# Four edits in a two-block transformer kernel: the rare places of a MoE expert inside its pair, earlier splits, one gate product, no GpSimd gemv

## The chip, the cores and the metric

The kernel runs on one core of one Trainium2 chip. The time is the device time of one execution in microseconds, the median of several. The core has a matrix engine (TensorE, PE in the profile, with its weight loads as PEld), a vector engine (DVE), a scalar engine (ACT), GpSimd (POOL) and a synchronisation engine (SP), which here issues nearly all loads. Each engine works off its own queue of instructions in order and waits on semaphores; 16 DMA engines move the data.

## What is computed

256 tokens of width 1024 pass two blocks of two layers each. Only the parts that the change touches are shown, in short:

```python
mod = c_act @ w_ada + b_ada                      # 6 x 1024 numbers for each layer
x = x + g1 * (mixer(norm(x)) @ w_out)            # layers of block 1: attention, convolution, spatial gating
x = x + g2 * peer_ffn(norm(x))                   # block 1: 16384 small experts, 8 heads x 16 chosen for a token
...
x = x + g1 * mix                                 # block 2: GLA in layer 0, LRU in layer 1
x = x + g2 * grouped_moe(norm(x))                # block 2: 16 experts of width 512, 2 for a token

def grouped_moe(h, ...):
    ...
    for e in range(16):
        he = silu(t @ w_gate[e]) * (t @ w_up[e])
        out = out + combine[:, e:e + 1] * (he @ w_down[e])
```

## The kernel before

The engines' queues are written out by hand: an instruction stands on its engine where the Python code calls it, and no scheduler moves it. Weights come through a `Stream`: `raw` and `fill` use slots of 1 MB, `release` gives one back and `pump` at once issues the next loads on SP (L71 and L74). Each load counts up one of eight semaphores (DMAHW0 to DMAHW7), so eight are in flight at most. For matmuls at full precision a weight is split into a high part (cast on ACT, L108) and a low part (subtraction on DVE, L113), and three matmuls are made. All matmuls are recorded at L267.

**Mixer and gemv.** The six vectors `mod` of a layer come from a product of the weights `in_ada` with one vector, in halves of 128x1024, by `gemv` (L321 to L333): one DVE instruction with a running sum (L333) for each half. For layer 0's parts 16 to 39, which are made while its first mixer runs, the first half of each of 12 tiles is instead multiplied on GpSimd (L330) and summed on ACT (L331). The first mixer runs the same code in both layers. Its DVE work begins with L609, and its output product is added to `x` at L474; then come a reciprocal (L414) and the scaled norm (L420, L433).

**PEER.** The 16384 experts are gone through in tiles of 128 by matmuls of split weights (`in_pdown`, then `in_pup`). Beside them a generator (`peer_select`) puts DVE and ACT work between the tiles: the choice of the experts, then 64 gate steps of four tokens. A step is a comparison of 128x1024 f16 (L970), two products of 128x512 (L976) that multiply the place's one-hot rows by their weights, matmuls of the result, and their evacuation (L944, L947).

**MoE.** Tokens are sorted to the 16 experts by one-hot matmuls. `experts` goes through eight pairs p of two experts, 64 places for each: loads of the gate weights (`in_mg`, four of 1 MB), up (`in_mu`) and down (`in_md`). In a pair: the gate half, the up half, `hidden`, the scatter of the pair before, `turn`, the down product, `parts`. Where an expert has over 64 tokens, blocks under `If(rv[p] > 64)` run the second 64 places: L1755 and L1758 behind the gate half, L1770 behind the up half, L1782 behind the down product. In the profiled run the block of L1782 is entered once in 16, in pair 2 of layer 1. After the eight pairs the scatter and `rstd` follow, and then, where an expert has over 128 tokens, L1826 would run the whole of `experts` again for the places from 128 and from 192, with a stream of its own (`S2`). No count here is over 128. Then `S.passed()` and `S.fill(1)` make the first two splits of the next stage (two L108, two L113).

An `If` is a branch on every engine that has instructions in the block. On the way around it an engine counts up the semaphores that the block would have counted up, and first waits for what the block's counts build on.

Of the kernel before, what the change touches and what calls it, by code (L numbers as in the profile page):

```python
# [7 lines left out]
F32 = mybir.dt.float32  # L8
# [4 lines left out]
OP = mybir.AluOpType  # L13
# [132 lines left out]


class LazyFour:


    def __init__(self, S):
        self.S, self.got = S, []

    def __getitem__(self, i):
        while len(self.got) <= i:
            self.got.append(self.S.raw())
        return self.got[i]


class Kern:  # L160
# [678 lines left out]
    def peer_select(self, qT, keys, st):  # L839
# [122 lines left out]
        for t0 in range(0, 256, 4):  # L962
# [3 lines left out]
            R = O[:, 0:512].rearrange("p (a j t) -> p a j t", a=2, t=2)  # L966
            C = O[:, 512:].rearrange("p (s a j t) -> p s a j t", s=2, a=2, t=2)
            bc = lambda i, n: (TT[:, t0 // 4, 4 * i:4 * (i + n)].rearrange("p (c t) -> p c t", t=2)[:, :, None, :]
                               .to_broadcast([128, 2 * n, 128, 2]))
            TX(O[:, :1024].rearrange("p (c j t) -> p c j t", c=4, t=2),  # L970
               self.io4[:, None, :, 0:2].to_broadcast([128, 4, 128, 2]), bc(0, 2), op=OP.is_equal)
# [3 lines left out]
            for n in (1, 0):  # L975
                TX(C[:, n], C[:, 0], bc(3 - n, 1), op=OP.mult)  # L976
# [518 lines left out]

    def route(self, h, hf, ht):
# [79 lines left out]
        cnt = self.sm.tile([1, 13], mybir.dt.int32, name="cnt")  # L1576
# [11 lines left out]
        def counts():  # L1588
            nc.vector.tensor_reduce(cnt[:, 0:8].rearrange("p (g b) -> p g b", b=2), swap(pr[0:1, 32:48]), op=OP.max, axis=AX)
            nc.vector.tensor_reduce(cnt[:, 8:12], pr[0:1, 32:48].rearrange("p (a b) -> p a b", b=4), op=OP.max, axis=AX)  # L1590
            nc.vector.tensor_reduce(cnt[:, 12:13], pr[0:1, 32:48], op=OP.max, axis=AX)
# [10 lines left out]
    def experts(self, S, base, ht, w, rk, g2, r, first=None):  # L1602
# [7 lines left out]
        P2 = self.fw6[:, :512].rearrange("p (t e s) -> p t e s", t=2, e=4)  # L1610
        PT2 = self.fw6[:, 512:768]
        if base:
            rk, old = self.scr(32), rk
            nc.vector.tensor_scalar(rk, old, float(-base), None, op0=OP.add)
        r3 = rk.rearrange("p (t e) -> p t e", t=2)
        w3 = w.rearrange("p (t e) -> p t e", t=2)
        xs = [t.bitcast(F32) for t in self.pair()]
        cw, cw2 = self.scr(8), self.scr(1)
        sg, he, hT, he2 = self.scr(512), self.scr(512), self.scr(512), self.scr(512)
        rv = None  # L1620
# [31 lines left out]
        def half(ws, x, c0):  # L1652

            ps = self.bank()
            for i in range(2):
# [5 lines left out]
                if first is None:  # L1661
                    for e in range(2):
                        S.release(ws[2 * i + e][0])
# [387 lines left out]
```

## Time and profile before

| | |
|---|---|
| median of three runs | 2714.59 us (2713.24 to 2715.59) |
| the profiled execution, its own time | 2714.08 us |
| its span, from the first to the last instruction | 2712.3 us |
| mean granted TensorE clock | 0.983 |
| busy: PE, DVE, ACT, POOL | 2567.9, 1892.2, 1173.2, 65.7 us |
| moved by the DMA engines | 658.32 MB, 243 GB/s in the mean |
| PEER of layer 0, then mixer 1 of layer 1 | about 165 to 980, to 1105 us |
| PEER of layer 1, then GLA | to 1915, to 2060 us |
| MoE of layer 0, LRU, MoE of layer 1 | 2075 to 2311, to 2420, 2440 to 2700 us |

Each row of the profile that follows names a line of the kernel, an engine and the tiles written and read; "idle before, releaser" is the time in which the engine did nothing ahead of it, and what ended that. SPq, PEq, DVEq and PEldq are the sequencers of the engines: their branches and semaphore waits, which are not counted as busy. The PE clock is in parts of full speed. The DMA share is the mean busy share of the 16 engines. A row of the windows has the window, its length, the busy time of PE, PEld, DVE, ACT and POOL (instructions in brackets), the PE clock, the DMA share and GB/s.

### The profile page before, as it was taken

How to read it: one execution, taken by the hardware profiler on the slowest of the kernel's cores; microseconds unless marked ns; L12 is line 12 of the kernel's file. 1: busy time of each engine (PE TensorE's matmuls, PEld its weight loads, DVE VectorE, ACT ScalarE, POOL GpSimd, SP SyncE). 2: the span in 40 equal slices, each digit the busy share in tenths (PEclk: the TensorE clock that was granted, in tenths of full speed). 3: DMA queues.
4: the chain of work that ended last, by engine and by line, in shares of the span. 5: the costliest groups of instructions: out<-in, count | busy, mean ns of one | idle time of the engine just before them, and what ended most of it. 6: DMA issues, size and time to landing. Idle time of an engine off the chain costs nothing. (4 is left out here: it accounts for less than half of the span.)

```text
span 2712.3 us, 42904 instructions
## 1 busy us (share of the span) xinstructions
PE 2567.9 (95%) x17017; PEld 2144.5 (79%) x17017; DVE 1892.2 (70%) x3505; ACT 1173.2 (43%) x1861; POOL 65.7 (2%) x62
## 2 busy tenths in 40 slices
PE   6899999999999999999999999999998998888997
PEld 5889999998888889999999888888895443874433
DVE  7868999996798977599899957888753121761222
ACT  3554555544544455454554345445643111651111
POOL 3300000000000000000000000000000000000000
PEclk8899999999999999999999999999999999999999
DMA  9562444445899963515444458988526999459795
GB/s 390 202 230 76 156 171 156 156 155 192 304 398 365 354 240 125 179 48 174 171 159 153 154 204 335 379 343 313 190 91 242 415 417 413 163 188 373 297 405 230
DMA packets 99812, 658.32 MB, mean 243 GB/s; under 512 B 11604, under 2 KB 13140, under 8 KB 26232
## 3 DMA queue, kind: packets, MB, share of 16 engines
q1 hardware_dynamic: 96480, 649.44, 62.9%
q10 hardware_dynamic: 3096, 5.68, 0.6%
q8 instruction: 154, 2.52, 0.4%
q14 instruction: 82, 0.67, 0.1%
HBM read 654.03 MB, written 1.05 MB: 242 GB/s over the span
## 5 line engine op out<-in xcount | busy, mean ns | idle before, releaser
L267 PE MATMUL bank<-hthi,whi 128*128 128x256 f32 x2920 | 848.2, 290 | 19.1 <-ACT whi L108 9.5
L267 PE MATMUL bank<-htlo,whi 128*128 128x256 f32 x2920 | 834.4, 286 | 5.6 <-DVE htlo L428 3.7
L267 PE MATMUL bank<-hthi,wlo 128*128 128x256 f32 x2920 | 832.1, 285 | 5.9 <-DVE wlo L113 5.8
L267 PEld LDWEIGHTS bank<-hthi,whi 128*128 128x128 f32 x2920 | 563.1, 193 | 32.1 <-ACT whi L108 9.7
L267 PEld LDWEIGHTS bank<-htlo,whi 128*128 128x128 f32 x2920 | 562.9, 193 | 11.1 <-DVE htlo L428 8.4
L267 PEld LDWEIGHTS bank<-hthi,wlo 128*128 128x128 f32 x2920 | 562.3, 193 | 8.0 <-DVE wlo L113 7.8
L108 ACT CAST whi<-r 128x1024 fp32r<-128x1024 f32 x331 | 347.4, 1050 | 486.9 <-PE bank L267 461.3
L113 DVE TENSOR_TENSOR wlo<-arena,whi 128x1024 fp32r<-128x1024 f32 (+1 forms) x322 | 392.3, 1222 | 199.4 <-ACT whi L108 194.5
L113 DVE TENSOR_TENSOR wlo<-r,whi 128x1024 fp32r<-128x1024 f32 x331 | 404.6, 1224 | 113.1 <-ACT whi L108 111.4
L108 ACT CAST whi<-arena 128x1024 fp32r<-128x1024 f32 (+1 forms) x322 | 332.7, 1037 | 306.8 <-PE bank L267 299.9
L267 PE MATMUL bank<-whi,hthi 128*128 128x512 f32 (+1 forms) x1088 | 421.7, 388 | 2.4 <-ACT hthi L306 2.4
L267 PE MATMUL bank<-wlo,hthi 128*128 128x512 f32 (+1 forms) x1088 | 421.8, 388 | 0.5 <-DVE wlo L113 0.5
L267 PE MATMUL bank<-whi,htlo 128*128 128x512 f32 (+1 forms) x1088 | 421.7, 388 | 0.2
L267 PEld LDWEIGHTS bank<-whi,hthi 128*128 128x128 f32 x1088 | 204.2, 188 | 43.9 <-ACT hthi L306 2.8
L267 PEld LDWEIGHTS bank<-whi,htlo 128*128 128x128 f32 x1088 | 204.2, 188 | 42.1 <-DVE htlo L307 1.1
L267 PEld LDWEIGHTS bank<-wlo,hthi 128*128 128x128 f32 x1088 | 204.2, 188 | 42.0 <-DVE wlo L113 1.1
L267 PE MATMUL bank<-arena 128*64 128x512 f32 (+6 forms) x856 | 176.0, 480 | 19.9 <-ACT arena L1674 12.4
L333 DVE SCALAR_TENSOR_TENSOR arena<-arena 128x1024 f32<-128x1024 f32 x136 | 163.6, 1240 | 0.0
L267 PEld LDWEIGHTS bank<-arena 128*64 128x64 f32 (+3 forms) x848 | 85.2, 165 | 85.6 <-issue 59.8
L1667 DVE SCALAR_TENSOR_TENSOR arena<-bank,arena 128x512 f32<-128x512 f32 x17 | 12.8, 752 | 176.4 <-PEq L1770 163.6
L947 DVE SCALAR_TENSOR_TENSOR arena<-bank,arena 128x416 f32<-128x416 f32 (+23 forms) x128 | 123.1, 962 | 0.0
L267 PE MATMUL bank<-arena,hthi 128*64 128x512 f32 x456 | 120.5, 595 | 2.2 <-ACTq L1782 0.8
(358 smaller groups left out, 2693.5 us busy)
## 6 DMA issues: line engine op xcount, KB each, us to landing
r<-in_pdown SPq DMA_DIRECT2D x110, 1024.0 KB, 4.9
arena<-in_pup SPq DMA_DIRECT2D x81, 1024.0 KB, 6.5
arena<-in_ada SPq DMA_DIRECT2D x72, 1024.0 KB, 6.9
arena<-in_mu SPq DMA_DIRECT2D x56, 1024.0 KB, 12.5
arena<-in_md SPq DMA_DIRECT2D x54, 1024.0 KB, 12.1
r<-in_pup SPq DMA_DIRECT2D x47, 1024.0 KB, 5.5
arena<-in_mg SPq DMA_DIRECT2D x40, 1024.0 KB, 11.5
r<-in_ada SPq DMA_DIRECT2D x24, 1024.0 KB, 7.0
```

Source lines behind the costliest of these rows:

```text
L108: k.nc.scalar.copy(hi[:, :n], ap)
L113: self.k.nc.vector.tensor_sub(lo[:, :n], ap, hi[:, :n].bitcast(F32))
L267: self.nc.tensor.matmul(o, l, r, start=start, stop=stop)
L333: self.nc.vector.scalar_tensor_tensor(w, w, 1.0, cb, op0=OP.mult, op1=OP.mult, accum_out=o)
L947: nc.vector.scalar_tensor_tensor(o[:, :, :j - j0], p4[:, :, j0:j], 1.0 / GSC, o[:, :, :j - j0], op0=OP.mult, op1=OP.mult)
L1667: nc.vector.scalar_tensor_tensor(o, pu, c, s, op0=OP.mult, op1=OP.mult)
```

## The change

There are four edits.

1. The block L1826 behind the pairs is gone. A new function `rest` computes the places over 128 of one pair's two experts, 128 at a time, with its own stream `S2` on the four slots that held the pair's down weights. It stands under `If(rv[p] > 128)` (L1824 of the changed kernel) inside the last block of each pair, `over(p)` (L1819 there, L1782 before). The other lines are L1792, L1795 and L1806 for L1755, L1758 and L1770. 12 counts are loaded into registers, not 13.
2. `S.passed()` and `S.fill(1)` move into `ahead()`, which is called in the last pair ahead of its down product. In layer 1 nothing is behind it to be split.
3. The gate step's two products become one of 128x1024, which reads one row block twice and writes two; the comparison writes the first and the third of three row blocks (L959, L963 for L970, L976).
4. `gemv` makes both halves on DVE (L321 for L333); the calls of GpSimd and ACT are not reached any more.

```diff
@@ gemv @@
-            self.gemv(l, m, cb, l == 0 and 16 <= m < 40)
+            self.gemv(l, m, cb)
@@ peer_select @@
-            R = O[:, 0:512].rearrange("p (a j t) -> p a j t", a=2, t=2)
-            C = O[:, 512:].rearrange("p (s a j t) -> p s a j t", s=2, a=2, t=2)
...
-            TX(O[:, :1024].rearrange("p (c j t) -> p c j t", c=4, t=2),
-               self.io4[:, None, :, 0:2].to_broadcast([128, 4, 128, 2]), bc(0, 2), op=OP.is_equal)
+            A = O.rearrange("p (s a j t) -> p s a j t", s=3, a=2, t=2)
+            R, C = A[:, 0], A[:, 1:3]
+            O2 = O.rearrange("p (s b) -> p s b", s=3)
...
+            TX(O2[:, 0::2], self.io4[:, None, :, 0:2].to_broadcast([128, 4, 128, 2]), bc(0), op=OP.is_equal)
             yield self.GC
             if len(pend) == 2:
                 evac(*pend.popleft())
-            for n in (1, 0):
-                TX(C[:, n], C[:, 0], bc(3 - n, 1), op=OP.mult)
+            TX(O2[:, 1:3], O2[:, 2:3].to_broadcast([128, 2, 512]), bc(2), op=OP.mult)
@@ experts @@
+        def rest(p, ws, o, x):
+
+            S2 = Stream(self, 3)
+            S2.free.extend(q for q, _ in ws)
+            self.add_rest(S2, l, p)
+            S2.pump()
...
+            for e in range(2):
+                c = 2 * p + e
+                nc.vector.tensor_scalar(rk2, r3[:, :, c:c + 1], -128.0, None, op0=OP.add)
...
+                def part():
+                    ps = self.bank()
+                    for i in range(2):
+                        q, v = S2.raw()
+                        for k in range(4):
+                            self.mm(ps, x[:, 4 * i + k, :], v[:, k * 512:(k + 1) * 512], i + k == 0, i + k == 4)
+                        S2.release(q)
+                    return ps
+
+                nc.scalar.activation(he2, part(), AF.Silu)
+                hidden(part(), cw2, he2, he2)
...
+                parts(y, o)
+                scatter(o, PT2)
...
             turn(he)
+            if p == 7:
+                ahead()
             ws = take()
             parts(down(ws), ys[p % 2])
-            if first is not None:
-                with over(p):
-                    turn(he2)
-                    o = ys[(p + 1) % 2]
-                    parts(down(ws), o)
-                    scatter(o, PT2)
+            with over(p):
+                turn(he2)
+                o = ys[(p + 1) % 2]
+                parts(down(ws), o)
+                scatter(o, PT2)
+                with self.tc.If(rv[p] > 128):
+                    rest(p, ws, o, x if j else x2)
+                    if j == 0:
+                        onehot(P2, 4 * g, 4, 64)
+                        gather(P2, x2)
             give(ws)
@@ moe @@
-        with self.tc.If(rv > 128):
-            S2 = Stream(self, 3)
-            S2.free.extend(S.lent[:2])
-            for base in (128, 192):
-                self.scr_at = [list(q) for q in at]
-                self.add_experts(S2, l)
-                S2.pump()
-                self.experts(S2, base, ht, w, rk, g2, r)
-        S.passed()
-        S.fill(1)
+        def ahead():
+            S.passed()
+            S.fill(1)
+
+        r = self.experts(S, l, ht, w, rk, g2, low, counts, weights, cnt, ahead)
```

The order of the instructions shows what this makes of the queues. SP, MoE of layer 0, around the last block of pair 6; in_md are the down weights of pair 7, in_lwin belongs to the LRU. Before:

```order
L74 DMA arena<-in_md 128x2048 [waits DMAHW7_49,PE_49]
L1782 COMPARE_AND_BRANCH
L1782 UNCONDITIONAL_BRANCH x2
L74 DMA arena<-in_md 128x2048 [waits DMAHW0_49,PE_49]
L74 DMA arena<-in_md 128x2048 [waits DMAHW1_49,PE_49]
L74 DMA arena<-in_md 128x2048 [waits DMAHW2_49,PE_49]
L74 DMA arena<-in_lwin 128x2048 [waits DMAHW3_49,PE_49]
L1758 COMPARE_AND_BRANCH
```

and the same place now, from the end of the block on (its twelve loads stand ahead of these rows):

```order
L74 DMA arena<-in_md 128x2048 [waits DMAHW2_49,PE_49]
L74 DMA arena<-in_md 128x2048 [waits DMAHW3_49,PE_49]
L1824 UNCONDITIONAL_BRANCH
L1824 UNCONDITIONAL_BRANCH [waits DMAHW0_49,DMAHW1_49,DMAHW2_49,DMAHW3_49,DMAHW4_49,DMAHW5_49,DMAHW6_49,DMAHW7_49]
L1819 UNCONDITIONAL_BRANCH [waits DMAHW0_49,DMAHW1_49,DMAHW2_49,DMAHW3_49,DMAHW4_49,DMAHW5_49,DMAHW6_49,DMAHW7_49]
L74 DMA arena<-in_md 128x2048 [waits DMAHW4_49,PE_49]
L74 DMA arena<-in_md 128x2048 [waits DMAHW5_49,PE_49]
L74 DMA arena<-in_md 128x2048 [waits DMAHW6_49,PE_49]
L74 DMA arena<-in_lwin 128x2048 [waits DMAHW7_49,PE_49]
L1795 COMPARE_AND_BRANCH
```

The way around L1782 had no wait on SP; each way around L1819 and L1824 now waits for all eight load semaphores, in every pair.

DVE, PEER of layer 0, two gate steps (L947/L935 is an evacuation, L113 the split of an expert tile, L1023/L1010 a product with the gates). Before:

```order
L970 TENSOR_TENSOR w_94<-io_88,TT 128x1024
L113 TENSOR_TENSOR wlo<-r_93,whi 128x1024
L1023 TENSOR_TENSOR arena<-arena,gt 128x2x108
L947 SCALAR_TENSOR_TENSOR arena<-bank,arena 128x4x86
L976 TENSOR_TENSOR w_94<-w_94,TT 128x512 x2
```

and now:

```order
L959 TENSOR_TENSOR w_94<-io_88,TT 128x2x512
L113 TENSOR_TENSOR wlo<-r_93,whi 128x1024
L1010 TENSOR_TENSOR arena<-arena,gt 128x2x108
L935 SCALAR_TENSOR_TENSOR arena<-bank,arena 128x4x86
L963 TENSOR_TENSOR w_94<-w_94,TT 128x1024
```

Nothing moves here but the two products, which are one.

DVE, the last pair of the MoE of layer 0, now (L462 is the scatter of pair 6, L295 evacuates the down product):

```order
L462 SCALAR_TENSOR_TENSOR x<-bank,adac_79,x 128x256 x8
L113 TENSOR_TENSOR wlo<-arena,whi 128x1024 x2
L295 TENSOR_TENSOR fa_19837<-bank,fa_19837 128x512 x2
L1819 COMPARE_AND_BRANCH
L295 TENSOR_TENSOR fa_19837<-bank,fa_19837 128x512 x2
```

Before, the two L113 stood behind L414 and L1826. The skipped part of L1819 grows on PE from some 40 instructions to some 240, on DVE from about 13 to 51, on ACT from 5 to 30. On DVE of the first mixer, layer 0, each L333 that had its other half on GpSimd is now two, four of them ahead of the first L609, seven between it and the first L474, and one between L414 and L420.

## Rows read from the trace of the kernel before

**Rows 1.** Windows, first PEER layer: us, busy (instructions) by engine, PEclk, DMA share, GB/s.
```profile
500.00:620.00 120.00, 116.56 (x1071) 113.84 (x1069) 118.55 (x185) 53.07 (x112) 0.00 (x0) 1.00 0.43 150
```

**Rows 2.** Waits of PE, whole run: engine, line, waited for, us in total, times, longest.
```profile
PE bank L267 <- DVE w L976: 12.3, 14, 3.2
```

**Rows 3.** Windows, first mixer of layer 0 and of layer 1.
```profile
76.40:154.50 78.10, 65.83 (x473) 61.31 (x473) 67.78 (x101) 39.32 (x93) 27.53 (x14) 0.85 0.53 198
1028.80:1089.20 60.40, 59.72 (x473) 56.28 (x472) 46.27 (x86) 32.04 (x79) 5.23 (x5) 0.92 0.34 123
```

**Rows 4.** Windows, MoE: layer 0, then layer 1 around pair 2.
```profile
2200.00:2230.00 30.00, 28.02 (x136) 10.67 (x138) 5.96 (x12) 2.93 (x5) 0.00 (x0) 1.00 1.02 418
2500.00:2530.00 30.00, 30.00 (x169) 14.70 (x166) 5.37 (x13) 3.33 (x6) 0.00 (x0) 1.00 0.74 283
2530.00:2560.00 30.00, 27.99 (x138) 10.86 (x138) 7.86 (x18) 4.12 (x7) 0.00 (x0) 1.00 0.65 247
```

**Rows 5.** Waits of PE in the MoE of layer 0, for loads.
```profile
PE bank L267 <- DMA arena<-in_mu: 2.2, 2, 1.4
PE bank L267 <- DMA wloraw<-in_mu: 1.6, 1, 1.6
```

**Rows 6.** Groups of DVE by shape, PEER of layer 0: busy us, mean ns, idle before.
```profile
L976 DVE TENSOR_TENSOR w<-w,TT 128x512 f16<-128x512 f16 x128 | 54.0, 422 | 2.2
L970 DVE TENSOR_TENSOR w<-io,TT 128x1024 f16<-128x1024 f16 x64 | 43.8, 685 | 0.2 <-PE bank L267 0.2
```

**Rows 7.** Timeline of DVE behind the first mixer: start, us, line, operation.
```profile
161.27 1.20 DVE L333 SCALAR_TENSOR_TENSOR r<-r,arena 128x1024 f32<-128x1024 f32 x1
162.40 0.08 DVE L333 DVE_READ_ACCUMULATOR r<-r,arena 128x1 f32 x1
```

**Rows 8.** Timeline of DVE, end of the MoE of layer 0.
```profile
2311.73 0.17 DVE L414 RECIPROCAL arena<-arena 128x2 f32<-128x2 f32 x1 [1.66 <-ACT arena L413]
2316.06 2.36 DVE L113 TENSOR_TENSOR wlo<-arena,whi 128x1024 fp32r<-128x1024 f32 x2 [4.17 <-DVEq L1826]
...
2319.10 0.87 DVE L433 SCALAR_TENSOR_TENSOR arena<-x,gs,bank 128x256 f32<-128x256 f32 x2 [0.59 <-PE bank L267]
```

**Rows 9.** Timeline of DVE, end of the MoE of layer 1.
```profile
2705.57 3.22 DVE L1916 SCALAR_TENSOR_TENSOR arena<-x,vec,bank 128x256 f32<-128x256 f32 x8 [4.60 <-PE bank L267]
```

**Rows 10.** SP's issues behind pair 6 of layer 0, and their us to landing.
```profile
2274.05 4.12 SPq L74 DMA_DIRECT2D arena<-in_md  x4
2280.34 3.96 SPq L74 DMA_DIRECT2D arena<-in_lwin  x3
...
arena<-in_md SPq DMA_DIRECT2D x1, 1024.0 KB, 17.4
arena<-in_lwin SPq DMA_DIRECT2D x1, 1024.0 KB, 17.3
```

**Rows 11.** Group of the page: the cast of a split.
```profile
L108 ACT CAST whi<-r 128x1024 fp32r<-128x1024 f32 x331 | 347.4, 1050 | 486.9 <-PE bank L267 461.3
```

**Rows 12.** Timeline of PE, the down product of pair 7, layer 0 and layer 1.
```profile
2294.30 7.09 PE L267 MATMUL bank<-arena 128*64 128x512 f32 x32 [0.74 <-ACT arena L1674]
...
2683.37 7.09 PE L267 MATMUL bank<-arena 128*64 128x512 f32 x32 [0.74 <-ACT arena L1674]
```

**Rows 13.** Instructions of L1826: count, ns min/median/max, first and last start.
```profile
L1826 SPq EVENT_SEMAPHORE  x16: 17/17/17, 2311.4 to 2682.9; - x16
...
L1826 PEldq COMPARE_BRANCH  x2: 3696/4868/6041, 2310.7 to 2699.7; - x2
```

**Rows 14.** Windows, SP's drain at L1826 in layer 0.
```profile
2312.00:2316.00 4.00, 0.00 (x0) 0.00 (x0) 0.00 (x0) 1.99 (x2) 0.00 (x0) 0.74 0.48 195
2316.00:2319.00 3.00, 1.99 (x7) 1.83 (x8) 2.44 (x3) 0.00 (x0) 0.00 (x0) 0.50 0.03 8
2319.00:2322.00 3.00, 3.00 (x15) 2.38 (x14) 2.66 (x7) 1.50 (x4) 0.00 (x0) 0.71 0.76 273
```

**Rows 15.** Waits of SP behind that drain.
```profile
SPq L74 <- DVE gs L420: 1.8, 1, 1.8
```

More of the change, by code (lines that the diff above doesn't have):

```diff
@@ L1600, in route, with experts @@
         return low, counts, weights, wp, rk, cnt
-    def experts(self, S, base, ht, w, rk, g2, r, first=None):
+    def experts(self, S, l, ht, w, rk, g2, low, counts, weights, cnt, ahead):
         nc = self.nc
@@ L1736, in experts @@
         onehot(Ps[0], 0, 4, 0)
-        if first is not None:
-            for i in (1, 2, 3):
-                first[0](i)
+        for i in (1, 2, 3):
+            low(i)
         gather(Ps[0], xs[0])
@@ L1747, in experts @@
             nc.scalar.activation(sg, ps, AF.Silu)
-            if p == 0 and first is not None:
-                first[1]()
-                first[2]()
-                rv = [nc.values_load(first[3][0:1, i:i + 1], min_val=0, max_val=256,
-                                     skip_runtime_bounds_check_because="a count of 256 tokens") for i in range(13)]
-            if first is not None:
-                if j == 0:
-                    with over(8 + g):
-                        onehot(P2, 4 * g, 4, 64)
-                        gather(P2, x2)
-                with over(p):
-                    nc.scalar.activation(he2, half(ws, x2, j * 128), AF.Silu)
-                    gather_w(P2, 4 * g, j, 1, cw2)
+            if p == 0:
+                counts()
+                weights()
+                rv = [nc.values_load(cnt[0:1, i:i + 1], min_val=0, max_val=256,
+                                     skip_runtime_bounds_check_because="a count of 256 tokens") for i in range(12)]
+            if j == 0:
+                with over(8 + g):
+                    onehot(P2, 4 * g, 4, 64)
+                    gather(P2, x2)
+            with over(p):
+                nc.scalar.activation(he2, half(ws, x2, j * 128), AF.Silu)
+                gather_w(P2, 4 * g, j, 1, cw2)
             give(ws)
@@ L1768, in experts @@
                 onehot(Ps[(g + 1) % 2], 4 * g + 4, 4, 0)
-            if first is not None:
-                with over(p):
-                    hidden(half(ws, x2, j * 128), cw2, he2, he2)
-                    transposed(P2, j, 1, PT2)
+            with over(p):
+                hidden(half(ws, x2, j * 128), cw2, he2, he2)
+                transposed(P2, j, 1, PT2)
             give(ws)
@@ L1778, in experts @@
             turn(he)
+            if p == 7:
+                ahead()
             ws = take()
             parts(down(ws), ys[p % 2])
-            if first is not None:
-                with over(p):
-                    turn(he2)
-                    o = ys[(p + 1) % 2]
-                    parts(down(ws), o)
-                    scatter(o, PT2)
+            with over(p):
+                turn(he2)
+                o = ys[(p + 1) % 2]
[3 more added lines that the diff above has]
+                    rest(p, ws, o, x if j else x2)
+                    if j == 0:
+                        onehot(P2, 4 * g, 4, 64)
+                        gather(P2, x2)
             give(ws)
@@ L1791, in experts @@
         scatter(ys[1], PTs[1][:, 1, :], ss)
-        self.rstd(ss, r)
-        return None if first is None else rv[12]
+        return self.rstd(ss)
     def moe(self, l, h, hf, g2):
```

70 lines of the change are left out of this document (43 added, 27 removed).

## Prediction

> **What bounds the kernel now.** I read the trace stage by stage, because the change touches three stages with different limits. First the busy time in a window of the first PEER layer, in which the gate steps run beside the expert matmuls, and what PE waits for there: DVE is busy 118.55 of 120 us and PE has lost 3.4 [rows 1]; PE's waits for a gate product are 12.3 us over both layers [rows 2]. DVE is the bound, barely. Second, the first mixer, which runs twice on the same work, in layer 0 with GpSimd multiplying beside it and in layer 1 without: from its first L609 to its first L474 it takes 78.1 us and 60.4 [rows 3]. In layer 1 PE is busy 59.72 us of that, so PE is the bound; in layer 0 DVE is busy 21.5 us longer and PE idles 12. Third, the MoE: the DMA engines are full (share 1.02, 418 GB/s) while PE is busy 28.02 of 30 us [rows 4] and has waited for loads only 2.2 + 1.6 us in the whole of layer 0 [rows 5]. Both are at their limit, and the loads have almost no lead over their use. Keep that in mind: what the DMA engines lose in this stage, PE soon loses too. The profiled run took 2714.08 us, its span 2712.3; the median of the runs is 0.5 us above it.
>
> **Gate product (two L976 become one).** The two products of a step take 422 ns each; the comparison L970 has 1024 f16 elements and takes 685 [rows 6]. One product of 1024 at L970's price saves 2 x 422 - 685 = 159 ns, and by an estimate 30 more for one start fewer: 0.19 us in each of 64 steps a layer. Some 45 of them lie in the saturated stretch: 8.5 us, more than the 6.2 us a layer that PE waits. The wait goes and no more, because then PE is the bound: **-12.3** for both layers. Bounds: -14, if the stretch itself quickens a little; and if the product with a repeated operand ran at the 1.20 us which an f32 operation of 1024 takes [rows 7], 0.36 us more per step, +32 for 45 steps twice.
>
> **Gemv.** GpSimd's and ScalarE's part goes; 12 L333 come to DVE in mixer layer 0 at 1.20 + 0.08 us [rows 7]. By the order four of them stand before the 78.1 us, seven inside, one behind. Inside: +9.0 of DVE work. Of the 21.5 us by which DVE is busier there than in layer 1, seven L333 that it has already make another 9.0; the other 12.5 are operations that take longer while GpSimd works, and they go. DVE's busy time so ends at 67.8 - 12.5 + 9.0 = 64.3 us, still above PE's 60: DVE is the bound, with 10.3 us of gaps now [rows 3], half of which I take as filled. The stretch then takes 64.3 + 5.2 = 69.5, 8.6 less. The four in front lie where PE is busy with the input product and cost an estimated 0.8 in all. The twelfth stands between the mixer and its norm beside the one at 161.27, 1.3 us of bare path. I take **-6.5**, between -12 (gaps all filled) and +3 (none filled, the four in front bare).
>
> **End of a MoE layer.** The skipped L1826 costs, from the reciprocal to the next scaling, 2319.10 - 2311.73 = 7.4 us in layer 0 [rows 8], of which about 1 is the chain's own: -6.4, with the two splits (2.36 us at 2316.06) inside it. In layer 1 DVE waits 4.60 [rows 9], about 0.8 of it its own: -3.8. The splits don't vanish: they move ahead of the evacuation of the last pair's down product. Their load, the first lwin, is issued at 2280.34 and takes 17.3 us, the last md (the end of the four issues that begin at 2274.05) at 2277.85 and 17.4 [rows 10]; so it lands 2.4 us later. A cast of 1.05 [rows 11] and the two subtractions, 3.4 us, follow, while the product is ready 1.8 us (a quarter of 7.09, [rows 12]) after the last md. Once PE waits for that md, the evacuation is held 2.4 + 3.4 - 1.8 = 4.0 us. Sum: -6.4 + 4.0 - 3.8 = **-6.2**. Bounds: -10.2 (splits hidden) and 0.
>
> **The If inside each pair.** This part decides. The loads of the rare case used to be issued inside L1826 alone, once a layer. Now they stand inside every pair's last If (L1819, nested L1824), and the way around it on SP has, as the order shows, waits for all eight load semaphores: SP can issue nothing until every load in flight has landed. L1826 did this twice; its 16 waits on SP lie between 2311.4 and 2682.9 [rows 13]. What one such drain costs is there to read: the DMA share falls from 2312 to 0.48, 0.03 and 0.76 [rows 14], which is 4 x 0.52 + 3 x 0.97 + 3 x 0.24 = 5.7 us lost; 1.8 of it SP waited for something else [rows 15]. So **3.9 us** each. Behind the waiting SP are queued the other md loads of the next pair and its mg loads, and PE waits for those. Bounds of one: 2.1 (the tail alone, 4 x 0.52) and 5.7.
>
> How many count? In layer 0 seven, pairs 0 to 6; behind pair 7's there are only loads of the LRU. Against them stands the lead at the end: the last md lands at 2277.85 + 17.4 = 2295.2, and its quarter of the product starts at 2294.30 + 5.3 = 2299.6 [rows 10, 12], 4.4 us: 7 x 3.9 - 4.4 = 22.9. In layer 1 pair 2 is the one whose block runs; PE is busy there without a gap and the DMA share falls to 0.74 and 0.65 [rows 4], so pairs 0 to 2 are absorbed. Pairs 3 to 6 count, against a lead of 2688.7 - 2682.9 = 5.8 by the same reckoning [rows 12, 13]: 4 x 3.9 - 5.8 = 9.8. Together **+32.7**; bounds 12.9 (at 2.1 each) and 52.5 (at 5.7).
> The Trainium skill, "DMA: Bandwidth & Descriptors", section "Anatomy of one DMA", gives a fixed cost of about 2.0 us per DMA, most of it completion, measured for DMAs of GpSimd. By it the drains would make 7 x 2.0 - 4.4 + 4 x 2.0 - 5.8 = 11.8, and the whole sum would come out near 2704. The row has in it also the spread of the 16 engines' ends, so I go by the row.
>
> **Longer skips.** The last If on PE now jumps over some 240 instructions where it was 40. A far jump took PE's sequencer 3.7 and 6.0 us at L1826, 4.9 in the mean [rows 13]. The sequencer reaches the branch while the 7.09 us of matmuls [rows 12] still run, and where PE then waits for loads the rest is covered; only pair 7 of a layer has no such cover. I take a quarter of the mean for these two: **+2.5**, between 0 and 15 skips at 2.4 (half of it) = 36. The jumps on DVE and ACT go with it; 12 counter loads instead of 13 are nothing.
>
> **Sum.** -12.3 - 6.5 - 6.2 + 32.7 + 2.5 = +10.2: 2714.1 + 10.2 = 2724.3, with the 0.5 to the median **2725 us**, slower by 0.4%. About 0.2%, 5.4 us, is what a measurement here can tell from no change.
>
> **Rivals.**
> *A drain costs its tail only* (2.1 us): the next loads' start overlaps the stragglers. Then +12.9 for the drains, in all -9.6: 2705. For it: nothing but eight short steps lies between the last landing and the next issue. Against it: [rows 14] shows 3 us with almost no transfer. The skill's 2.0 us would lead to the same. 0.15.
> *The drains are hidden anyway*: PE, at 28 of 30 us with waits for ACT and DVE besides, is the real bound. Then the other parts alone, with the splits hidden: -12.3 - 6.5 - 10.2 + 2.5 = -26.5: 2688. For it: 3.8 us of load waits in a layer [rows 5]. Against it: a share of 1.02 leaves no room to catch up. 0.10.
> *PE's skips are bare*: with the queues full, code comes later than at L1826. From the point where the fetch outlasts the matmuls still queued, each pair pays; at 1.6 us in 15 pairs, +24 instead of 2.5: 2746. Against it: it would fall into the same waits as the drains. 0.12.
> *The wide product is slow* (1.20 us): +32 instead of -12.3: 2769. Against it: L970 repeats an operand too and is fast. 0.04.
> The forecast has the remaining 0.59, in itself from 2707 to 2742.
>
> **How the numbers follow.** The range 2696 to 2747 takes in the forecast with its bounds of drain, the cheap drain and the bare skips; it leaves out the hidden drains and the slow product. Slower (above 2720): 0.40 of the forecast's 0.59, 0.12 and 0.04, in all 0.56. Faster (below 2709.2): the hidden drains 0.10, most of the cheap drain 0.13, and 0.04 of the forecast, 0.27. The same: the rest, 0.17.
>
> **What would show it.** In the changed profile: SP's own waits at L1819 and L1824 in every pair, over 100 us in both layers; a DMA share below 0.95 in the MoE windows, with a hole after each drain; PE waiting for in_mg, in_mu and in_md some 25 us in layer 0 against 3.8; pairs of about 34 us. The gate step's wait gone from PE's waits; mixer layer 0 at about 70 us; no 7.4 us from reciprocal to scaling at the end of the MoE. The forecast is wrong if the MoE windows keep a share of 1.0, or if SP is past its waits long before the last load lands.

## The result, and the profile of the changed kernel

| | before | changed |
|---|---|---|
| median, us | 2713.91 (2712.57 to 2715.59) | 2739.77 (2734.67 to 2748.68) |
| ratio | | 1.0093, 95% interval 1.0079 to 1.0108 |
| profiled execution: span, us | 2712.3 | 2745.6 |
| its mean granted TensorE clock | 0.983 | 0.978 |

The change makes the kernel 25.9 us slower; 10.2 were forecast. The profiled execution of the changed kernel is the longest of its four, so its stages stand about 9 us above the median.

**The stages.** I compare the time at which one instruction of each stage starts in the two profiled executions. From the norm behind the first mixer to the last product of PEER, the first PEER layer gives 3.9 us back and the second 4.0; the first mixer with its norm 2.3; GLA loses 1.6. The MoE of layer 0, from PE's first matmul behind the blocks of its first gate half to the reciprocal, takes 261.0 us for 229.6, and behind it 6.4 are won; the MoE of layer 1, by the same marks, loses 20.8 and then wins 3.8. Nearly all of the loss is in the two MoE layers.

The windows of that stretch of layer 0, before, changed, and without the skipped block (the experiment e1_no_rest, below); columns as in [rows 1].
```profile
2082.10:2311.70 229.60, 206.93 (x1079) 96.17 (x1079) 50.08 (x105) 29.09 (x52) 0.20 (x1) 1.00 1.01 413
```
```profile
2072.70:2333.70 261.00, 222.80 (x1081) 103.63 (x1081) 52.44 (x108) 30.90 (x54) 0.20 (x1) 0.95 0.90 360
```
```profile
2071.30:2300.90 229.60, 207.25 (x1081) 96.38 (x1081) 52.44 (x107) 31.11 (x54) 0.20 (x1) 1.00 1.01 414
```
Two losses show at once. The DMA share falls from 1.01 to 0.90, as forecast for the drains. The granted clock falls from 1.00 to 0.95, and this no part of the forecast had.

The instructions of the last If (L1819) in the changed kernel, as [rows 13] show them of L1826: count, ns min/median/max, first and last start; and SP's waits there in layer 0 and layer 1 (us in total, times, longest).
```profile
L1819 SPq EVENT_SEMAPHORE  x120: 17/17/17, 2083.6 to 2724.5; - x120
...
L1819 PEldq COMPARE_BRANCH  x16: 73/6116/6316, 2086.3 to 2724.1; - x16
```
```profile
SPq L1819 <- SPq L1819: 118.0, 46, 7.6
...
SPq L1819 <- SPq L1819: 101.0, 23, 16.5
```
SP drains its queue in each of 15 pairs: 120 waits, eight each. PE's sequencer takes 6.1 us in the median for a branch that took 0.337 before (73 is the one pair that enters the block, and does not jump):
```profile
L1782 PEldq COMPARE_BRANCH  x17: 73/337/357, 2095.6 to 2686.0; - x17
...
L1782 PEldq EVENT_SEMAPHORE  x15: 51/51/51, 2100.1 to 2690.5; - x15
```

What PE waits for in the MoE of layer 0 now, beside the 2.2 and 1.6 us of [rows 5]:
```profile
PE bank L255 <- DVEq L1795: 8.5, 4, 2.3
PE bank L255 <- PEq L1819: 7.3, 3, 3.0
PE bank L255 <- ACT arena L1663: 5.7, 8, 0.7
PE bank L255 <- DVEq L1819: 3.7, 1, 3.7
PE bank L255 <- PEq L1795: 3.6, 6, 1.7
PE bank L255 <- issue: 3.3, 1, 3.3
PE bank L255 <- DMA arena<-in_md: 2.5, 2, 1.4
```
The waits stand at branches, not at loads. A wait for several semaphores is put down to the last of them, so the rows name the place, pair by pair behind L1819, and not safely the culprit; the experiments had to tell it.

The other places. The gate product, first PEER layer, by shape, and what PE waits for there (before: 6.1 us in this layer, of the 12.3 of [rows 2]); the window that answers to [rows 1], and the stretch of the first mixer in layer 0 from its first L597 to its first L462, which answers to the first of [rows 3]:
```profile
L959 DVE TENSOR_TENSOR w<-io,TT 128x1024 f16<-128x1024 f16 x64 | 44.0, 687 | 1.2 <-PE bank L255 1.1
L963 DVE TENSOR_TENSOR w<-w,TT 128x1024 f16<-128x1024 f16 x64 | 43.9, 687 | 0.0
```
```profile
PE bank L255 <- DVE w L963: 3.1, 2, 2.6
```
```profile
500.00:620.00 120.00, 116.89 (x1087) 115.11 (x1086) 118.30 (x162) 53.20 (x115) 0.00 (x0) 1.00 0.45 158
77.27:149.60 72.33, 63.69 (x473) 58.85 (x471) 62.56 (x117) 31.07 (x79) 5.80 (x6) 0.88 0.55 199
```
The product costs 687 ns, L970's price as taken; the further 30 ns that were to fall away with one start stand in no row. DVE is as busy as before (118.30 us for 118.55), and half of PE's wait stays.

DVE at the end of the MoE, as [rows 8] and [rows 9]: layer 0, then layer 1.
```profile
2333.65 0.17 DVE L402 RECIPROCAL root<-root 128x2 f32<-128x2 f32 x1 [1.66 <-ACT root L401]
2334.62 0.87 DVE L421 SCALAR_TENSOR_TENSOR arena<-x,gs,bank 128x256 f32<-128x256 f32 x2 [0.74 <-PE bank L255]
...
2739.01 3.22 DVE L1949 SCALAR_TENSOR_TENSOR arena<-x,vec,bank 128x256 f32<-128x256 f32 x8 [0.80 <-PE bank L255]
```
The 7.4 us from the reciprocal to the first scaling are 1.0, and the 4.60 are 0.80.

### The profile page after: what moved, and what is told of

The parts are those of the page before. It is cut to its first block, busy times and chain, and to the rows that moved or that the text cites. A ratio compares the mean times of both kernels' runs of the same rounds, so it can differ in the third digit from the quotient of the medians.

```text
span 2745.6 us, 42858 instructions
## 1 busy us (share of the span) xinstructions
PE 2590.7 (94%) x17017; PEld 2155.7 (79%) x17017; DVE 1866.0 (68%) x3399; ACT 1160.7 (42%) x1837; POOL 31.5 (1%) x50
## 3 DMA queue, kind: packets, MB, share of 16 engines
q1 hardware_dynamic: 96480, 649.44, 62.6%
## 5 line engine op out<-in xcount | busy, mean ns | idle before, releaser
L113 DVE TENSOR_TENSOR wlo<-arena,whi 128x1024 fp32r<-128x1024 f32 (+1 forms) x322 | 387.5, 1207 | 206.1 <-ACT whi L108 205.3
L113 DVE TENSOR_TENSOR wlo<-r,whi 128x1024 fp32r<-128x1024 f32 x331 | 403.3, 1220 | 127.8 <-ACT whi L108 126.6
L321 DVE SCALAR_TENSOR_TENSOR arena<-arena 128x1024 f32<-128x1024 f32 x144 | 171.0, 1226 | 0.0
L255 PE MATMUL bank<-arena,htlo 128*64 128x512 f32 x368 | 115.1, 622 | 18.5 <-DVEq L1795 8.5
## 6 DMA issues: line engine op xcount, KB each, us to landing
arena<-in_mg SPq DMA_DIRECT2D x40, 1024.0 KB, 11.8
```

The costliest lines, as they stand in the source:

```text
L113: self.k.nc.vector.tensor_sub(lo[:, :n], ap, hi[:, :n].bitcast(F32))
L255: self.nc.tensor.matmul(o, l, r, start=start, stop=stop)
L321: self.nc.vector.scalar_tensor_tensor(w, w, 1.0, cb, op0=OP.mult, op1=OP.mult, accum_out=o)
```

## The experiments

Two theories stood against each other. **Drains**: SP's waits starve PE of weights, and the long jump is covered. **Skips**: PE's jump over 240 instructions ends after the matmuls queued ahead of it, and every pair pays. The diffs are against the changed kernel unless said otherwise; "e1" is e1_no_rest.

### Taking the block apart

**e1_no_rest**: the pair's last block without the places over 128.
```diff
-                with self.tc.If(rv[p] > 128):
-                    rest(p, ws, o, x if j else x2)
...
```


> The changed kernel without the block under If(rv[p] > 128): the places over 128 of an expert are left out. Every other edit stays. Both theories, the drain of SP and the longer skips, expect the whole loss to go: from the stage times of the changed kernel the gate product gave 8, the mixer 2.3 and the ends of the MoE about 10 us, so some 2694 us (2690 to 2700). SP's waits at L1819 and a PE branch of 6 us there should both be gone. If a part of the loss lies elsewhere (splits held in pair 7, GLA), it stays above 2700.

Measured: 2691.77 us, ratio to before 0.9913 (0.9896 to 0.9930). So the block that is never entered costs 2739.77 - 2691.77 = 48.0 us, and the other edits win 23.9 against the 2715.66 us of the kernel before as measured beside e1. The profile has pairs of 30.3 and 28.3 us by turns again, as before.

**e3_loads_only**: the block holds its 12 loads and no work. SP drains, PE's jump is short.
```diff
-                    rest(p, ws, o, x if j else x2)
...
+                    S2 = Stream(self, 3)
+                    S2.free.extend(q for q, _ in ws)
+                    self.add_rest(S2, l, p)
+                    S2.pump()
+                    for _ in range(12):
+                        S2.release(S2.raw()[0])
```


> The block under If(rv[p] > 128) holds only its twelve loads, no work (the places over 128 are left out). SP's way around has the eight waits, the jumps of PE, DVE and ACT are as short as before. Drain theory: 25 to 35 us above e1, near the changed kernel; DMA share about 0.9 in the MoE. Skip theory: within 3 us of e1. Mixed: 15 to 25 above e1.

Measured: 2727.44 us, 1.0042 (1.0027 to 1.0056): 35.7 over e1.
```profile
L1819 SPq EVENT_SEMAPHORE  x120: 17/17/17, 2082.7 to 2706.8; - x120
...
L1819 PEldq COMPARE_BRANCH  x16: 73/334/352, 2085.2 to 2706.4; - x16
```
By the profiled execution, which is 37.4 us longer than e1's, the eight pairs of layer 0 take 22.7 us more than in e1 (from the start of one down product to that of the next), those of layer 1 take 7.0 more, and the end of layer 0 a further 6.1: pair 7's product waits for its last loads (9.8 us for 7.1), then its evacuation is held behind the two splits (PE stands 3.72 us for 1.60), and the lower clock takes the remaining 1.3. The splits wait for the first lwin. PE's branch is at its 0.334 us, and the clock over the whole run is 0.984.

**e2_rest_no_loads**: the block keeps its matmuls and vector work, but takes the pair's own weights; no load, so no drain.
```diff
-            S2 = Stream(self, 3)
...
+            turn_ws = iter(list(ws) * 3)
...
-                        q, v = S2.raw()
+                        _, v = next(turn_ws)
```


> The block under If(rv[p] > 128) keeps its matmuls, vector work and length, but its weights are the four down tiles that the pair holds, not loads of its own (the places over 128 would come out wrong). The way around has no waits of SP, the jumps of PE, DVE and ACT are as long as in the changed kernel. Drain theory: as without the block, within 3 us of e1. Skip theory: all of the loss stays, 2735 to 2740. Mixed, as the pairs' +2.3 us in the first pairs suggest: 12 to 18 us above e1.

Measured: 2722.36 us, 1.0024 (1.0012 to 1.0036): 30.6 over e1, in both layers alike (pairs +16.8 and +15.3). Drain and skip are each nearly as dear alone; together they cost 48.0, not 66.3.

### Which engine's skip

**e5_pe_only**: the block holds 200 matmuls and nothing else.
```diff
-                    rest(p, ws, o, x if j else x2)
...
+                    for _ in range(50):
+                        ps = self.bank()
+                        for f in range(4):
+                            self.mm(ps, hT[:, f * 128:(f + 1) * 128], ws[f][1][:, 0:512], f == 0, f == 3)
```


> The block under If(rv[p] > 128) holds 200 matmuls and nothing else (the places over 128 are left out), so PE's jump is about as long as in the changed kernel, those of DVE, ACT and SP as short as in e1. If PE's jump is the cost of e2 (30.6 us above e1): 20 to 30 us above e1 (2712 to 2722), with PE branches of 6 us at L1819. If it is the jumps of DVE and ACT: within 3 us of e1.

**e6_vec_only**: 40 DVE and 25 ACT instructions instead.
```diff
+                    for _ in range(40):
+                        nc.vector.tensor_scalar(rk2, r3[:, :, 2 * p:2 * p + 1], -128.0, None, op0=OP.add)
+                    for _ in range(25):
+                        nc.scalar.copy(PT2, P2[:, 0, 0:4, :].rearrange("p e s -> p (e s)"))
```


> The block under If(rv[p] > 128) holds 40 small instructions of DVE and 25 copies of ACT and nothing else (the places over 128 are left out). PE's jump is short, those of DVE and ACT are as in the changed kernel. If PE's jump is the cost of e2: within 3 us of e1 (2689 to 2695). If DVE's and ACT's: 20 to 30 above it. A share of both: 5 to 15.

**e8_pe_short**: as e5_pe_only with `range(12)`, 48 matmuls.

> The block under If(rv[p] > 128) holds 48 matmuls and nothing else (the places over 128 are left out): about twice the jump of the kernel before, a quarter of the changed one's addition. If the cost has a threshold, that the target must be fetched anew once it is far enough: either 0.34 us at the branch and no loss (within 2 us of e1), or 6 us and the loss of e5. If it grows with the length: a quarter of e5's loss, 5 to 8 us.

Measured: 2716.69 (1.0010, 1.0000 to 1.0020), 2691.33 (0.9922, 0.9906 to 0.9939) and 2694.36 (0.9926, 0.9910 to 0.9943): 24.9, -0.4 and 2.6 over e1. The kernel before took 2713.47 us beside these three and 2715.66 beside e1, so -0.4 and 2.6 are not clear of nothing, and 24.9 is. It is PE's jump that costs, 24.9 of e2's 30.6, and not those of DVE and ACT by themselves; where e2's other 5.7 lie was not traced. The cost doesn't grow in proportion: a quarter of the matmuls costs a tenth. PE's branch of L1819 in e5_pe_only, then in e8_pe_short:
```profile
L1819 PEldq COMPARE_BRANCH  x16: 73/6002/6257, 2085.7 to 2690.4; - x16
```
```profile
L1819 PEldq COMPARE_BRANCH  x16: 73/337/3312, 2083.2 to 2673.1; - x16
```
Over 48 matmuls the branch takes 0.337 us, once 3.3; over 200 it takes 6.0 in nearly all pairs. What it does in that time stands in the DMA view. First the window of the first far jump in e5_pe_only (branch from 2085.7, window to 2092.2), then that of a near jump in e1 (0.34 us from 2115.1, window to 2121.1):
```profile
q1 hardware_dynamic: 380, 2.74, 100.6%
q8 instruction: 1, 0.02, 0.9%
```
```profile
q1 hardware_dynamic: 346, 2.49, 99.9%
q8 instruction: 1, 0.02, 1.1%
```
Each brings one packet on the instruction queue, behind a queue of loads that is full (the near jump of e1's first pair, 0.2 us, brings none). Both packets start some 3.6 to 3.8 us behind the start of the branch and have landed 1.0 to 1.1 us later. The near branch has long ended by then. The far one ends at 2091.7, 1.4 us behind the landing of its packet, which lies in this window (2089.2 to 2090.3):
```profile
q1 hardware_dynamic: 54, 0.43, 96.1%
q8 instruction: 1, 0.02, 5.6%
```
The rule holds without an exception here: in the fourteen traces PE's sequencer takes over 1.5 us for 80 branches behind 2040 us, and every one ends 1.3 to 1.7 us behind the landing of such a packet. So a near jump stays in code that the sequencer has, and a far one waits for code to be loaded. Over the run that queue moves 150 packets in e1, 162 in e8_pe_short, 173 in e5_pe_only, 175 in the changed kernel.

Now the cover. In the kernel before, the branch of the first pair starts at 2095.6 and PE's semaphore wait behind it at 2100.1: the sequencer has 4.5 us to spare, so a branch of 6.0 ends 1.5 too late. Part of that was idle time already, since PE waits at the join for the other engines as well. In the first seven pairs of layer 0 the gaps there are 0.78 to 1.56 us in e1, 9.1 in sum, and 1.85 to 2.09 in e5_pe_only, 13.7 in sum: +4.5. Once PE then stops in the middle of a product with nothing to wait for, 3.2 us of matmuls behind the gap:
```profile
2249.92 0.65 PE L255 MATMUL bank<-arena,htlo 128*64 128x512 f32 x2 [2.50 <-issue]
```
By the same sign this too is a wait for code: a packet of the instruction queue lies between 2247.3 and 2248.4, 1.5 us ahead of the next matmul. The five stops of over 1.2 us in the MoE of all kernels that are put down to "issue" (one in e2, one in e5, two in the changed kernel, one in e12) all end 1.3 to 1.5 us behind such a packet, and the kernels whose jumps in the pairs are near have none. With these 2.5 and one stretch of 3.4 us at about half clock behind the second gap, 1.7, that makes 8.7 of the 9.6 us by which e5_pe_only's stretch of layer 0 (239.2 us) is longer than e1's.

PE behind the first pair's skip in layer 0, from the timelines of e1, e5_pe_only and the changed kernel (in brackets the idle time ahead):
```profile
2090.70 0.64 PE L255 MATMUL bank<-whiraw,hthi 128*64 128x512 f32 x1 [1.41 <-DVEq L1819]
```
```profile
2091.97 0.61 PE L255 MATMUL bank<-whiraw,hthi 128*64 128x512 f32 x1 [1.86 <-DMA arena<-in_mu]
```
```profile
2092.76 0.99 PE L255 MATMUL bank<-whiraw,hthi 128*64 128x512 f32 x1 [2.05 <-PEq L1819]
2093.54 1.06 PE L255 MATMUL bank<-whiraw,hthi 128*64 128x512 f32 x1
```
In the changed kernel PE stood 2.05 us, and the matmuls behind it take 1.06 us where they took 0.59 to 0.64. The windows behind the skip show why, e1 first, then the changed kernel behind pairs 0, 1 and 2:
```profile
2090.70:2094.10 3.40, 3.40 (x16) 1.20 (x18) 0.00 (x0) 0.00 (x0) 0.00 (x0) 1.00 1.02 424
```
```profile
2092.70:2096.10 3.40, 3.34 (x8) 1.16 (x10) 0.00 (x0) 0.00 (x0) 0.00 (x0) 0.52 0.40 164
...
2126.80:2130.20 3.40, 3.40 (x10) 1.19 (x8) 0.00 (x0) 0.00 (x0) 0.00 (x0) 0.53 0.60 236
2157.60:2161.00 3.40, 3.40 (x10) 1.21 (x8) 0.00 (x0) 0.00 (x0) 0.00 (x0) 0.52 1.01 412
```
The granted clock is 0.52, the lower of the engine's two levels (1.2 of 2.4 GHz), and 8 to 10 matmuls fit where 16 did. PE had been idle 2.05, 2.17 and 2.20 us ahead of these, with the gap's end up to 1.3 us before the fall; behind the 1.41 to 1.56 us of e1 it stays at 1.00. Where the clock falls, 3.4 us at about half of it cost 1.7 us besides the gap. But the length of a gap does not decide it alone. Behind pair 5 of the changed kernel PE stood 2.30 us, longer than in any of the three, and the clock stayed:
```profile
2254.80:2258.20 3.40, 3.34 (x16) 1.43 (x18) 0.00 (x0) 0.00 (x0) 0.00 (x0) 1.00 1.01 417
```
In layer 1 it stayed behind gaps of 2.05, 2.09, 2.20 and 2.23 us and fell behind another of 2.23. What else decides it was not found.

### How full queues matter

**e12_half_loads**: e5_pe_only with every load into a 1 MB slot cut to half its columns.
```diff
-                self.k.nc.sync.dma_start(ap, src)
+                w = n // 2 if raw == 2 else n
+                self.k.nc.sync.dma_start(ap[:, :w], src[:, :w])
```


> As e5 (200 matmuls in the rare block), but the expert weights that go to slots of 1 MB are loaded only by half (the results are wrong by that), 4 of 12 MB in a pair less, so that the DMA engines are no longer full in the MoE. If PE's far jump is long because its code is fetched behind the loads: branches at L1819 well below e5's 6.0 us, 3.5 to 4.5 in most pairs, and the pairs near e1's 28.3 and 30.3 us instead of some 31 each. If the fetch takes 6 us whatever the DMA engines do: still 6.0, and the pairs as in e5.

Measured: one execution, 2672.51 us. The first window is a pair of layer 0 in e5_pe_only, the second in this kernel; then its branch:
```profile
2130.00:2160.00 30.00, 26.42 (x134) 11.18 (x132) 6.27 (x14) 2.94 (x5) 0.00 (x0) 1.00 1.01 408
```
```profile
2130.00:2160.00 30.00, 26.95 (x137) 11.11 (x138) 6.27 (x14) 2.94 (x5) 0.00 (x0) 1.00 0.82 277
```
```profile
L1820 PEldq COMPARE_BRANCH  x16: 3376/3930/6039, 2085.1 to 2648.2; - x16
```
With the DMA share down from 1.01 to 0.82 the same jump takes 3.9 us in the median, under the 4.5 to spare, and the pairs take 30.4 and 28.6 us by turns, close to e1's. Since loads arrive sooner here too, the pair times alone would not prove it; the branch's own duration does. It is not one duration but a spread from 3.4 to 6.0, and the packet's place gives it: the branch of 3.39 us from 2115.5 has its packet in this window (2116.5 to 2117.5), with nothing else on the DMA engines:
```profile
q8 instruction: 1, 0.02, 6.0%
```
It starts 1.0 us behind the branch, for 3.4 to 4.1 in the far jumps of all pairs but the last in the three kernels that jump over 200 matmuls and more with full loads (the changed one, e2 and e5). So full queues delay the start of the load of code, and with it the end of the jump, by some 2.5 us.

### The single edits, against the kernel before

**e4_gate_only**: its diff is that of `peer_select` in the change; nothing else.

> The kernel before with the one gate product alone. The forecast's term: -12.3 us (2701.6). By the changed kernel's stage times: 4.0 us in each PEER layer, -8 (2706), with 3.1 us of PE's wait for L963 left in each layer and the rest of the stretch bound by PE.

**e10_gemv_only**: nothing but this line.
```diff
-            self.gemv(l, m, cb, l == 0 and 16 <= m < 40)
+            self.gemv(l, m, cb)
```


> The kernel before with all of gemv on DVE and nothing else. The forecast's term: -6.5 us (2707). By the changed kernel's stage times up to the norm behind the first mixer, -2.3 to -3.5: 2710 to 2712. If GpSimd's share was no burden: 2 to 6 us slower than before.

Measured: 2705.41 us, 0.9963 (0.9949 to 0.9976), and 2709.93, 0.9984 (0.9974 to 0.9995). In the stages of e4_gate_only the two PEER layers get 4.1 and 4.4 us shorter.

### One block for all pairs

If each pair pays for its own jump, one If a layer should cost one. All three kernels below count up the largest of the 16 counts as a 13th number and run `rest` for all eight pairs under it, at different places of pair 7. Here the diff of e7_one_if; the other two stand elsewhere and hand `rest` other scratch tiles:
```diff
+            if p == 7:
+                with self.tc.If(rv[12] > 128):
+                    for q in range(8):
+                        rest(q, ws, ys[0], x)
```
**e7_one_if**: behind the last block of pair 7.

> The three other edits kept, and the places over 128 of all eight pairs under one If of the largest count, in pair 7 behind its last block, where the down matmuls are still queued and no MoE load is left to issue. One long jump and one drain a layer instead of eight. By the measured loss of 30.6 us for 15 jumps, 2 us each, and a drain that holds only loads of the LRU: 2 to 6 us a layer above e1, 2696 to 2704, faster than the kernel before. If one jump there costs as L1826 did at the end, 7 and 4 us: 2703.

**e9_if_early**: ahead of pair 7's `turn`, with scratch tiles of its own and the up slots kept back.

> As e7, the places over 128 of all pairs under one If a layer, but that If stands in pair 7 between the scatter of pair 6 and the turn ahead of the down product: PE still has the up half's matmuls queued, and DVE is idle there. The four slots of the up weights are given back behind it, not ahead. If the cost of a jump is the code fetch beyond what PE has queued (6.0 against 4.5 us): 1.5 to 3 us a layer above e1, 2694 to 2698, below e7 by 7 to 10. If a jump this long costs the same wherever it stands: as e7, 2703 to 2706.

**e11_if_behind_up**: directly behind pair 7's up half, with the gate slots kept back.

> As e9, with the one If a layer moved once more: directly behind the up half of pair 7, ahead of that pair's block L1806, with scratch of its own and the gate weights' slots, so that no other If has let PE's queue run empty just before. If the cost of a jump is the fetch beyond the queued matmuls, 1.5 us in layer 0 and in layer 1 each, and the end of each MoE stays as in e1: 2694 to 2698. If it stays near 2705, a jump over this much code can't be covered by matmuls.

Measured: 2704.78 (0.9964, 0.9953 to 0.9976), 2706.16 (0.9965, 0.9951 to 0.9978) and 2705.90 (0.9955, 0.9940 to 0.9970). All three are 13 to 14.4 us above e1 and beat both kernels; none comes near the 2694 to 2698 that I had hoped the earlier places would give. The jump and PE's wait behind it, in e7_one_if and in e11_if_behind_up:
```profile
L1826 PEldq COMPARE_BRANCH  x2: 3332/4864/6397, 2290.6 to 2680.3; - x2
...
PE bank L255 <- DVEq L1826: 11.9, 2, 7.2
```
```profile
L1810 PEldq COMPARE_BRANCH  x2: 5614/5790/5966, 2276.1 to 2666.9; - x2
...
PE bank L255 <- DVEq L1810: 9.2, 2, 5.8
```
Wherever the one If stands, PE loses some 5 us at it twice: at the join it waits for the other engines' sequencers too, which have jumped as far. In e7_one_if DVE's branch is recorded with 56 ns, but the semaphore behind it comes 5.4 us later in layer 0 and 3.0 in layer 1:
```profile
L1826 DVEq COMPARE_BRANCH  x2: 56/56/56, 2292.0 to 2681.6; - x2
...
L1826 DVEq EVENT_SEMAPHORE  x2: 21/21/21, 2297.4 to 2684.6; - x2
```
PE's 11.9 us there are nearly all of the 12.7 by which this profiled execution is longer than e1's. In e11_if_behind_up DVE's branch comes 4.6 us behind PE's, and its jump takes 5.5 and 3.0 us, so the matmuls queued on PE at PE's own branch had run out before DVE was past it; the rest of the loss in e9_if_early and e11_if_behind_up was not traced. None of the counts is over 128 in these inputs, so what the block costs when it is entered was not measured in any kernel.

## Why the prediction was right in direction and wrong in size

**Gate product: half right.** The price per step (687 ns for the 685 taken, [rows 6]) and the place were right. That the whole wait goes was wrong: 3.1 of 6.1 us in layer 0 stay, and -12.3 is -8.5 by the stages of e4_gate_only (its median is 10.3 us below that of the kernel before, with an interval from 6.5 to 13.8, which by itself does not exclude the forecast). DVE is busy 118.30 of 120 us now, for 118.55 [rows 1], so the stretch stays DVE's; that DVE uses the time won to come further ahead in its own queue is my reading, no row shows it.

**Gemv: sign right, size about half.** From the first L597 to the first L462 the stretch takes 149.6 - 77.3 = 72.3 us for 78.1 [rows 3], where 69.5 was forecast; in the twelve kernels with this edit it takes 71.2 to 72.3. DVE's share of it was right: DVE is busy 62.56 us there, for 64.3 forecast, so the 12.5 us charged to GpSimd did go. What did not come is the half of the gaps: DVE still idles 72.3 - 62.6 = 9.7 us, for 10.3 before. The first L597 comes 0.9 later, as priced for the four in front. From the first L462 to the norm 11.1 us stand for 8.5, a further 1.3 over what the twelfth L321 was priced at. Net: -2.3 for -6.5 in this execution and -5.1 in that of e10_gemv_only; by the medians e10_gemv_only gives 0.16% (0.05 to 0.26), some 4 us.

**End of a layer: right.** -6.4 and -3.8 came to the tenth [rows 8, 9]. The held splits were over-priced: of the 6.1 us at the end of layer 0 in e3_loads_only, the hold of the evacuation is 2.1 (3.72 - 1.60), for 4.0. They are late because of the drains: in e1 the same splits cost nothing (its stretch is 229.6 us, as before).

**Drains: right in the sum.** Forecast 22.9 in layer 0, 9.8 in layer 1 and 4.0 for the splits, 36.7 in all; e3_loads_only, which has the drains alone, lost 35.7 by the medians, and in its profiled execution 22.7 and 7.0 in the pairs and 6.1 at the end of layer 0. Pair by pair it came otherwise than read, so the 3.9 us of [rows 14] are not shown as the price of each drain. In layer 0 the seven steps from one down product to the next grow by 0, 0, 1.2, 2.3, 8.6, 2.2 and 8.4 us, and in layer 1 all 7.0 come in the last step. That the sum came so close is in part luck. The Trainium skill, "DMA: Bandwidth & Descriptors", section "Anatomy of one DMA", gives about 2.0 us for a DMA of GpSimd; an estimate by it would have been 11.8 + 4.0 = 15.8 with the splits. The measurement lies at the row's sum and not at this one.

**Longer skips: here it failed.** "Where PE then waits for loads the rest is covered; only pair 7 of a layer has no such cover": +2.5. The runs show 24.9 for PE's jump alone, 30.6 with the block's other work, and 48.0 - 35.7 = 12.3 on top of the drains. I had set the 4.9 us mean of [rows 13] against the 7.09 us of matmuls [rows 12], though the sequencer reaches the branch only 4.5 us ahead of its end. I had also taken a mean over two jumps which differ for a reason: 6.0 us with full queues, 3.7 with empty ones. Nearly every pair behaves like the first: 14 of the 16 branches in the changed kernel took 5.9 to 6.3 us. The rival "PE's skips are bare", +24, was the right mechanism and was given 0.12. That its +24 met the 24.9 of e5_pe_only is partly luck: its 1.6 us in each pair are made up otherwise than it said, of 0.65 more of gap, a stop for code, and the clock. Its objection, that the jump falls into the same waits as the drains, is half true and depends on the layer. Over e1, by the profiled executions: layer 0 lost 28.8 us with drains, 16.8 with skips, 31.3 with both; all behind it 8.3, 15.7 and 22.7. In layer 0, where the drains starve PE, they cover nearly all of the skip. In layer 1, where they are absorbed, the two add up.
On the branch itself the Trainium skill, "Advanced Engine Details and Errata", section "Control Flow Timing", has some 108 ns for a compare-and-branch. The rows show 73 ns for the one that isn't taken, 337 for the near jump and 6116 for the far one; only the first is near the page's figure, and the measurement decides.

**The clock: a term that was missing.** Mean clock and span of the profiled executions give the time lost to the lower level: 2745.6 x 0.022 = 60.4 us in the changed kernel, 2690.3 x 0.017 = 45.7 in e1, so some 15 of the 55.3 us between these two. In the stretch of layer 0 alone it is 12 to 13 of 31.4 (261.0 x 0.05, the share being rounded). It comes with the skips and needs no drains: e3_loads_only has no such loss (0.984), and e2_rest_no_loads, which has no drains, has some (0.981); its gaps behind the jump are 1.9 to 2.7 us in layer 0. Since gaps of one length are followed by a fall or not, this loss is measured and not explained to the end.

**The sum, with what was measured:** gates -7.9 (stages of the changed kernel), gemv -2.3, ends -10.2 without the held splits, GLA +1.6, the block with all its effects +48.0: +29.2, for a measured +25.9. Some of the signs that the prediction named came: SP's waits (118.0 and 101.0 us, over 100 forecast), a share of 0.87 to 0.97 in eight of the nine windows of 30 us in layer 0, the end at 1.0 us. Others did not: PE does not wait "for in_mg, in_mu and in_md some 25 us", the time stands at branches and in a lower clock; the pairs of layer 0 take 29.6 to 34.8 us, 32.3 in the mean, for about 34; half of the gate step's wait is left; and mixer layer 0 is at 72.3.

**Open.** GLA's 1.6 us come with the gemv edit, though nothing of that edit is near it: e4_gate_only does not have them, e10_gemv_only does (92.75 us from one reciprocal to the next for 91.16), with the same instructions at a lower clock. GLA in the kernel before, then in e10_gemv_only:
```profile
1923.30:2014.40 91.10, 88.79 (x596) 78.86 (x596) 47.53 (x67) 49.49 (x81) 0.00 (x0) 0.98 0.26 94
```
```profile
1916.80:2009.60 92.80, 90.49 (x597) 80.51 (x597) 47.55 (x68) 49.56 (x82) 0.00 (x0) 0.96 0.27 92
```
Why the clock stays low longer there is open. Between 48 and 200 matmuls no length of the jump was tried. A kernel whose block loads on another queue, so that SP doesn't drain, was not tried with the full block.

## What to carry to other kernels

A branch around a rare case is not free because it is never entered: read what each engine does on the way around it, its semaphore waits and the length of the jump in code, and compare the jump with the time from the sequencer's arrival to the end of its queued work, not with that work's whole length. Rare code that is spread over every iteration pays this every time; gathered under one If a layer (e7_one_if) it pays once a layer, and beat both kernels. Where two costs share a wait, price both alone and then ask, stage by stage, which of them is hidden by the other.

## What the runs showed of the hardware that I had not expected

- A jump of TensorE's sequencer takes 0.334 to 0.337 us in the median over 40 to some 90 instructions and 6.0 over 200 and more with full DMA queues; 3.4 to 6.0 at a share of 0.82, 3.3 to 3.7 where the queues are empty. A long one ends 1.3 to 1.7 us behind the landing of a packet of 0.02 MB on the instruction queue, in all 80 cases; the packet starts some 1.0 us behind the branch with empty queues and 3.4 to 4.1 with full ones. A near jump can bring such a packet too, but its branch doesn't wait for it.
- Behind a far jump PE can stop again in the middle of straight code, 2.5 to 3.3 us, until 1.3 to 1.5 us after the next such packet (five cases).
- Jumps of DVE and ACT over 40 and 25 more instructions cost nothing that could be told from noise (e6_vec_only, -0.4 us). Over eight copies of `rest` DVE's takes 3.0 and 5.4 us (e7_one_if), in the time behind a branch that is itself recorded with 56 ns.
- The lower clock followed gaps of 2.05, 2.17 and 2.20 us on PE in the changed kernel, and a fourth of 2.11 only once a stop of 3.32 came behind it; it did not follow one of 2.30 there, nor gaps of 1.41 to 1.56 in e1. In e5_pe_only, of the first four (1.86, 2.07, 1.90, 2.09) it followed the second alone.
- The clock also moves single executions: the four of the changed kernel lie at 2734.67 us with a clock of 0.983 and at 2738.90 to 2748.68 with 0.978 to 0.979.
